# A hybrid attention and S5 block on one core: parameter scratch beside the query tiles, eigenvalue powers in the S5 stage, modulation weights two loads ahead

## The chip, the cores and the metric

The kernel runs on one core of one Trainium2 chip. The metric is the device time of one execution in microseconds (us). The core has a matrix engine (TensorE, PE in the profile), a vector engine (VectorE, DVE), a scalar engine (ScalarE, ACT), a general engine (GpSimd, POOL), a sync engine (SyncE, SP) that here only issues transfers, and 16 DMA engines that all queues share.

## The reference, cut to what matters

Two layers work on 512 latent and 256 context tokens of width 1024. Layer one is a latent attention with 16 heads, a SiLU gate and a residual norm. Layer two is a bidirectional S5 state-space layer with a gated linear unit. Each layer is modulated by a condition vector: shift, scale and gate come from a product of the silu of the condition with `w_mod`.

```python
sh, sc, gt = jnp.split(cond @ w_mod[i] + b_mod[i], 3, axis=-1)
h_lat = x * (1.0 + sc[:, None]) + sh[:, None]
# layer 1 (S5), for each direction, 128 groups, 64 states
lam_dt = lam * dt[:, None]
lam_bar = jnp.exp(lam_dt)
b_bar = ((lam_bar - 1.0) / lam)[..., None] * bmat
# x[t] = lam_bar * x[t-1] + b_bar u[t];  y[t] = Re(C x[t])
```

The kernel takes eight tokens as one step of the S5 recurrence. It therefore needs the powers 0 to 8 of `lam_bar` for tables, and the powers 8, 16, 32, 64 and 128 for a tree over the context.

## The kernel before

All matrix products are three products of a high and a low part (`mm3`, L81 to L83). The stages in order of time are these.

**Front, 0 to about 62 us.** Four times (q = 0 to 3) `mod_part` (L576) multiplies six loads of layer one's modulation weights, and `h_make` (L597 to L602) then makes two of the eight input tiles (`hh`, `hl`). The list `wtile` names the buffer of each weight load: 16 loads go to buffers of `hh` and `hl`, seven to `M`, one to `pair`. Beside it `s5_params` runs on DVE and then on POOL. Its scratch (`arena`, `T1`, `keep`) lies in the tiles `Qh0`, `Qh1`, `Ql0`, `Ql1` and one tile `G`; its scratch `T2` lies in `ext`. On POOL it builds the powers 0 to 8 (`cmul`, six instructions of 128x128 at L237 to L242, sixteen times), and then the four higher powers by squaring (four more `cmul`), negated copies (L292) and five stores `lamd` (L293). After that the two `bk` tiles, which lie in `ext` as well, are cleared (L629).

**Gating, about 62 to 361 us.** The loop over m = 0 to 15 makes `gate(m)` (48 matmuls against `hh`, `hl`), and between gates it places other work. `tables(n)` builds n chunks of S5 tables, 20 of 32 (`S5IN`) in this stage. A chunk is ten POOL instructions: six on 128x512 that make `wo` (L356 to L361), two that make `b1`, `b2` (L366, L368) and two that write `bk` (L372). One chunk later come the chunk's lag products on PE (L325, L328, called the lag here), which read `wo` and `bk`; their result `ks` is stored in eight small transfers `kd` on SP's queue. The chunk's input `cb` is loaded on the same queue, one chunk ahead, into two buffers. `s5_coefs` (L301) turns the powers on PE at m = 1, and right behind it `queries()` makes `Qh`, `Ql` from `qd`. `mod_more`, called from m = 2 on, three times per m, loads the next 512 to 768 KB of modulation weights (`pair`, two buffers, on ACT's queue) and runs the step of the load before it (L103), 24 steps in all. `prep(0)` for the first head is placed at m = 11 to 15.

**Attention, about 361 to 800 us.** Sixteen heads of five units; the other 12 chunks are built in it, five per eight units, and then 32 input tables on POOL (L391 to L396).

**Output product, S5, GLU, final product, to 1746 us.** In S5 `lamt` is loaded from `lamd` and used by `tree` (L1197 to L1202) and `recur` (L1212). POOL has no work there.

The order on each engine is made ahead of time by a planner that runs the program against a cost model. In this trace the users of the PSUM tiles `mm` (gates, lags, turns) stand on PE in the order in which the program names them; the steps L103 write other PSUM tiles (`modps`) and stand ahead of where the program has them.

Of the kernel before, what the change touches and what calls it, by code (L numbers as in the profile page):

```python
# [9 lines left out]
F32 = mybir.dt.float32  # L10
F32R = mybir.dt.float32r
I32 = mybir.dt.int32
AF = mybir.ActivationFunctionType
ALU = mybir.AluOpType
# [4 lines left out]
P = 128  # L19
D = 1024  # L20
KC = D // P
TL, TC = 512, 256
T = TL + TC
# [8 lines left out]
def hybrid_mla_s5(ctx, tc, I, O):  # L32
# [7 lines left out]
    def f(ap):  # L40
        return ap.bitcast(F32)
# [104 lines left out]
    G, Gd = [], {}  # L146


    GR, NCH, S5IN, WO = 128, 32, 20, [3]
    lamd = dram.tile([P, 5, 3, GR], F32, name="lamd")  # L150
    pind = dram.tile([8, GR, 2, P], F32, name="pind")
# [3 lines left out]

    def s5_params(take, take2, T2, pw, cci):

        def slots(k, take=take):
            return take()[:, :k * GR].rearrange("p (s g) -> p s g", g=GR)

        arena = [slots(6) for _ in range(3)]
        n = [0]
# [23 lines left out]
        A, S, M = ALU.add, ALU.subtract, ALU.mult  # L186
        T1, keep = slots(6), slots(6)

# [46 lines left out]

        def cmul(dr, di, ar, ai, br, bi, t1, t2, eng=pool):
            eng.tensor_tensor(t1, ar, br, op=M)  # L237
            eng.tensor_tensor(t2, ai, bi, op=M)
            eng.tensor_tensor(dr, t1, t2, op=S)
            eng.tensor_tensor(t1, ar, bi, op=M)  # L240
            eng.tensor_tensor(t2, ai, br, op=M)
            eng.tensor_tensor(di, t1, t2, op=A)  # L242

        lre, lim, lbr, lbi, cr, ci = (keep[:, i, :] for i in range(6))
        dt, den = cr, T2[:, 4, :]
# [29 lines left out]
        cps = [cps[k // 3][:, 2 * (k % 3):2 * (k % 3) + 2, :] for k in range(8)]  # L275
        lt = [arena[l // 2][:, 3 * (l % 2):3 * (l % 2) + 3, :] for l in range(5)]
        pk = [T1[:, 1:3, :], T1[:, 3:5, :], T2[:, 3:5, :]]
        p = pk[0]
        pool.memset(p[:, 0, :], 1.0)
        pool.memset(p[:, 1, :], 0.0)  # L280
        for k in range(8):
            pool.tensor_copy(pw[0:64, :, k, :], p[0:64])
            pool.tensor_copy(pw[64:128, :, 7 - k, :], p[64:128])
            cmul(cps[k][:, 0, :], cps[k][:, 1, :], p[:, 0, :], p[:, 1, :], clr, cli, t1, t2)
            q = lt[0] if k == 7 else pk[(k + 1) % 3]
            cmul(q[:, 0, :], q[:, 1, :], p[:, 0, :], p[:, 1, :], lbr, lbi, t1, t2)
            p = q
        for l in range(1, 5):
            a = [lt[l - 1][:, 0, :], lt[l - 1][:, 1, :]]
            cmul(lt[l][:, 0, :], lt[l][:, 1, :], *a, *a, t1, t2)  # L290
        for l in range(5):
            pool.tensor_scalar_mul(lt[l][:, 2, :], lt[l][:, 1, :], -1.0)  # L292
            pool.dma_start(out=lamd[:, l], in_=lt[l])  # L293
        return cps
# [121 lines left out]
    with ExitStack() as ctx_:  # L416
# [119 lines left out]
        with mkpool(name="in_h", bufs=KC) as hp, mkpool(name="in_w", bufs=3) as wp, \  # L536
# [17 lines left out]

            wtile = iter(["hh", "hl"] * KC + ["M"] * 7 + ["pair"])
            gmes = ExitStack()
# [63 lines left out]

            names = iter(("Qh0", "Qh1", "Ql0", "Ql1", "G"))

            def place():
                n = next(names)
                return (gv if n == "G" else qkv).tile([P, T], F32, name=n)
            cps = s5_params(place, lambda: gv.tile([P, T], F32, name="G"),
                            ext[:, 3 * GR:].rearrange("p (s g) -> p s g", g=GR), pw, cci)
# [109 lines left out]
            dve.tensor_sub(Cl, ckv, f(Ch))  # L737

            Qh, Ql = [], []

            def queries():
                for i in range(2):
                    Qh.append(qkv.tile([P, T], F32R, name=f"Qh{i}"))
                    Ql.append(qkv.tile([P, T], F32R, name=f"Ql{i}"))
                    dve.tensor_copy(Qh[i], qd[i])
                    dve.tensor_sub(Ql[i], qd[i], f(Qh[i]))
            rows1, steps1 = mod_steps(1, 0, 384, pair, ps, work, 0)
# [11 lines left out]
            def mod_more():  # L759

                n = next(done)
                ends.get(n - 2, lambda: None)()
                if ready:
                    ready.pop()()
                for load, step in itertools.islice(steps, 1):
                    load()
                    ready.append(step)
            todo = iter(range(S5IN))

            def tables(n):  # L770
                for c in itertools.islice(todo, n):
                    chunk(s5in, mm, c, S5IN - 1)
            prep0 = dict(zip(range(11, HEADS), prep(0)))
            for m in range(HEADS):
                for _ in gate0 if m == 0 else gate(m):
                    if m >= 2:
                        mod_more()
                if m >= 2:
                    mod_more()
                if m == 1:  # L780
                    s5_coefs(cps, mm, t512)
                    queries()
                for fn in prep0.pop(m, ()):
                    fn()
                tables(2 if m == 0 else 1 + (m % 4 == 2))
            spill()
# [350 lines left out]
    lamt = stp.tile([P, 5, 3, GR], F32, name="lamt", bufs=1)  # L1137
    sp.dma_start(out=lamt, in_=lamd)

    ues, (up,) = pools(dict(name="u_s", bufs=2))  # L1140
    us, scs = {}, {}

    def u_tile(m):
# [396 lines left out]
```

## Time and profile before

| what | us |
|---|---|
| three timed runs | 1749.81, 1754.17, 1759.38 |
| median | 1754.17 |
| profiled execution, its own time | 1748.03 |
| its span, first to last instruction | 1746.0 |
| PE busy in it | 1560.3 (89%) |
| POOL busy in it | 650.2 (37%) |

The span is cut in 40 slices of 43.65 us in the page's second part, with the busy share of each engine in tenths. A wait is put down to what released it. Spans of POOL are rough, and ends of matmuls are modelled.

### The profile page before, as it was taken

The numbers are of one execution on the slowest core, as the hardware profiler recorded it, in microseconds if no ns is written. First come the engines' busy times: TensorE is split into PE (matmuls) and PEld (weight loads), VectorE is DVE, ScalarE is ACT, GpSimd is POOL, SyncE is SP. The second block draws the span as 40 slices with busy tenths as digits, with TensorE's granted clock in tenths as the row PEclk, the third lists the DMA queues.
The fourth block names the chain that finished last, engine by engine and source line by source line (L and its number), as shares of the span: only waits on it lengthen the run. The fifth ranks groups of instructions, "written<-read, shape, count | busy, mean of one in ns | idle before, by whom it ended". The sixth has DMA issues, their size and how long they took to land.

```text
span 1746.0 us, 26883 instructions
## 1 busy us (share of the span) xinstructions
PE 1560.3 (89%) x9870; PEld 1305.9 (75%) x9870; DVE 962.8 (55%) x2502; ACT 729.9 (42%) x1253; POOL 650.2 (37%) x686
## 2 busy tenths in 40 slices
PE   6925978889889889999999999999779999999997
PEld 4713856678778778888888999888568888888876
DVE  7441322347758778785453488899853333333336
ACT  2411211246556556674224766766563222222220
POOL 3997777969948889970000000000000000000022
PEclk7966989999989999999999999999889999999999
DMA  9245676453356665654326767487452333333342
GB/s 326 79 139 185 209 230 201 137 194 120 115 159 196 203 193 195 200 181 158 115 69 196 240 221 233 141 333 282 155 212 89 119 108 108 109 108 109 135 155 73
DMA packets 156733, 293.60 MB, mean 168 GB/s; under 512 B 55069, under 2 KB 86217, under 8 KB 155577
## 3 DMA queue, kind: packets, MB, share of 16 engines
q1 hardware_dynamic: 104112, 235.84, 40.4%
q10 hardware_dynamic: 52104, 55.03, 10.4%
q8 instruction: 78, 1.28, 0.3%
q0 software_dynamic: 384, 1.01, 0.2%
q14 instruction: 55, 0.44, 0.1%
HBM read 230.39 MB, written 69.55 MB: 172 GB/s over the span
## 4 chain that ended last, share of the span: by engine, by line
PE 57%; DMA 14%; DVE 12%; POOL 6%; ACT 5%; issue 3%; SPq 2%; ACTq 0%; DVEq 0%; POOLq 0%
PE mm L81 16%; PE mm L83 16%; PE mm L82 16%; PE mm L1167 3%; DMA pair<-in_w_mod_dram 3%; DMA wraw<-in_wout_dram 2%; DMA cb<-in_CB_dram 1%; DMA toed<-kd 1%; DMA pw<-in_Bc_dram 1%; PE tr L858 1%; DMA ext<-pind 1%; DVE wlo L65 1%; DMA wraw<-in_win_dram 1%; PE modps L103 1%; POOL wo L359 1%
## 5 line engine op out<-in xcount | busy, mean ns | idle before, releaser
L65 DVE TENSOR_TENSOR wlo<-wraw,whi 128x1024 fp32r<-128x1024 f32 (+1 forms) x155 | 178.5, 1153 | 338.4 <-ACT whi L65 336.7
L1404 POOL TENSOR_TENSOR x<-x,row_g 128x1024 f32<-128x1024 f32 x4 | 11.3, 2829 | 926.0 <-DMA x<-x1d 926.0
L65 ACT CAST whi<-wraw 128x1024 fp32r<-128x1024 f32 (+1 forms) x155 | 149.2, 964 | 397.2 <-PE mm L82 262.9
L81 PE MATMUL mm<-st,whi 128*128 128x512 f32 x512 | 204.5, 399 | 5.4 <-ACT st L76 5.2
L83 PE MATMUL mm<-st,wlo 128*128 128x512 f32 x512 | 202.4, 395 | 0.0
L82 PE MATMUL mm<-st,whi 128*128 128x512 f32 x512 | 201.0, 393 | 0.5 <-DVE st L77 0.5
L81 PE MATMUL mm<-h,whi 128*128 128x512 f32 (+1 forms) x384 | 138.6, 362 | 0.2 <-DVE bnmv L950 0.2
L82 PE MATMUL mm<-h,whi 128*128 128x512 f32 (+1 forms) x384 | 137.1, 358 | 0.8 <-DVE h L1110 0.8
L83 PE MATMUL mm<-h,wlo 128*128 128x512 f32 (+1 forms) x384 | 136.6, 356 | 0.0
L81 PE MATMUL mm<-hh,whi 128*128 128x512 f32 (+1 forms) x320 | 113.4, 366 | 8.1 <-ACT whi L65 4.6
L81 PEld LDWEIGHTS mm<-st,whi 128*128 128x128 f32 x512 | 97.4, 190 | 26.8 <-ACT st L76 6.4
L82 PEld LDWEIGHTS mm<-st,whi 128*128 128x128 f32 x512 | 97.3, 190 | 23.2 <-DVE st L77 1.5
L83 PEld LDWEIGHTS mm<-st,wlo 128*128 128x128 f32 x512 | 97.2, 190 | 22.7
L82 PE MATMUL mm<-hl,whi 128*128 128x512 f32 (+1 forms) x320 | 113.0, 355 | 0.0
L83 PE MATMUL mm<-hh,wlo 128*128 128x512 f32 (+1 forms) x320 | 111.4, 352 | 0.0
L834 ACT ACTIVATE p<-sc,mx 128x768 f32<-128x768 f32 (+1 forms) x96 | 73.5, 766 | 37.7 <-DVE mx L833 35.3
L65 DVE TENSOR_TENSOR ptl<-tr,pth 128x384 fp32r<-128x384 f32 (+1 forms) x160 | 79.1, 524 | 15.4 <-ACT pth L65 14.5
L65 ACT CAST pth<-tr 128x384 fp32r<-128x384 f32 (+1 forms) x160 | 68.9, 462 | 40.9 <-PE tr L858 34.2
L833 DVE TENSOR_REDUCE mx<-sc 128x1 f32<-128x768 f32 (+1 forms) x96 | 73.8, 771 | 15.6 <-PE sc L823 14.4
L81 PEld LDWEIGHTS mm<-h,whi 128*128 128x128 f32 x384 | 72.9, 190 | 11.9 <-issue 0.7
L82 PEld LDWEIGHTS mm<-h,whi 128*128 128x128 f32 x384 | 73.1, 190 | 10.9 <-DVE h L1110 1.1
L83 PEld LDWEIGHTS mm<-h,wlo 128*128 128x128 f32 x384 | 72.9, 190 | 10.4
(377 smaller groups left out, 4188.0 us busy)
## 6 DMA issues: line engine op xcount, KB each, us to landing
wraw<-in_wglu_dram SPq DMA_DIRECT2D x64, 512.0 KB
wraw<-in_win_dram SPq DMA_DIRECT2D x36, 512.0 KB
wod<-wo SPq DMA_DIRECT2D x32, 512.0 KB
pw<-in_Bc_dram SPq DMA_DIRECT2D x32, 512.0 KB
pt<-wid SPq DMA_DIRECT2D x32, 512.0 KB
wo<-wod SPq DMA_DIRECT2D x32, 512.0 KB
pair<-in_w_mod_dram ACTq DMA_DIRECT2D x16, 768.0 KB
wo<-pind SPq DMA_DIRECT2D x21, 512.0 KB
```

Source lines behind the costliest of these rows:

```text
L65: return act.copy(hi, src).ins, (eng or dve).tensor_tensor(lo, src, f(hi), op=ALU.subtract).ins
L81: pe.matmul(ps, lh, rh, start=first, stop=False)
L82: pe.matmul(ps, lh, rl, start=False, stop=False)
L83: pe.matmul(ps, ll, rh, start=False, stop=last)
L103: pe.matmul(mps[32 * j:32 * j + 2, :n], sT[:, kc, :], w[:, n * j:n * j + n], start=(kc == 0), stop=(kc == KC - 1))
L359: pool.tensor_tensor(wi, cr, pi, op=ALU.mult)
L833: dve.reduce_max(mx[:, 1:2], s, axis=AX.X, negate=True)
L834: act.activation(p[:, a:b], s, AF.Exp, bias=mx[:, 1:2], scale=1.0, accum_out=mx[:, 2:3])
L858: pe.transpose(tp[:, n, :], p[:, j * P:(j + 1) * P], ident)
L1167: pe.matmul(o[:, r, 96 * q:96 * (q + 1)], wi[:, q, r, :], us[m][:, 4 * (c % 2) + q, :], start=True, stop=True)
L1404: pool.tensor_tensor(x, x, rows["g0"], op=ALU.mult)
```

## The change

- `s5_params` gets another place for its scratch: `T1` and the kept values lie in three tiles of `ls` (`xp0`, `xp1`, `xp0`), the arena in `Qh0`, `Qh1`, `Ql0`. One tile `G` less is taken.
- On POOL only the power 8 is stored, by one transfer. The powers 16 to 128 and the negated copies are made in the S5 stage, on POOL, from the loaded power 8, with a new scratch tile `lsc`.
- `Qh`, `Ql` are made in line, ahead of the loop over m.
- `wtile` names four loads for `hh`, `hl` and then a cycle of seven `M` and two `pair`, so that buffers of `M` and `pair` are used again within the front.
- `mod_more` is called from m = 0 on, and a step runs two loads after its own.
- `S5IN` is 19; `tables` builds none at m = 0, then one per m and one more at m = 3, 7, 11, 15. `s5_coefs` moves to m = 4.

```diff
-    GR, NCH, S5IN, WO = 128, 32, 20, [3]
-    lamd = dram.tile([P, 5, 3, GR], F32, name="lamd")
+    GR, NCH, S5IN, WO = 128, 32, 19, [3]
+    lamd = dram.tile([P, 2, GR], F32, name="lamd")
...
-        T1, keep = slots(6), slots(6)
+        X = [slots(4, take4) for _ in range(3)]
+        T1 = X[0]
...
-        lre, lim, lbr, lbi, cr, ci = (keep[:, i, :] for i in range(6))
+        lre, lim, cr, ci, lbr, lbi = (X[1 + i // 4][:, i % 4, :] for i in range(6))
...
-        lt = [arena[l // 2][:, 3 * (l % 2):3 * (l % 2) + 3, :] for l in range(5)]
-        pk = [T1[:, 1:3, :], T1[:, 3:5, :], T2[:, 3:5, :]]
+        pk = [T1[:, 1:3, :], X[2][:, 2:4, :], T2[:, 3:5, :]]
...
-            q = lt[0] if k == 7 else pk[(k + 1) % 3]
+            q = pk[(k + 1) % 3]
...
-        for l in range(1, 5):
-            a = [lt[l - 1][:, 0, :], lt[l - 1][:, 1, :]]
-            cmul(lt[l][:, 0, :], lt[l][:, 1, :], *a, *a, t1, t2)
-        for l in range(5):
-            pool.tensor_scalar_mul(lt[l][:, 2, :], lt[l][:, 1, :], -1.0)
-            pool.dma_start(out=lamd[:, l], in_=lt[l])
+        pool.dma_start(out=lamd, in_=p)
...
-            wtile = iter(["hh", "hl"] * KC + ["M"] * 7 + ["pair"])
+            wtile = itertools.chain(["hh", "hl"] * 2, itertools.cycle(["M"] * 7 + ["pair"] * 2))
...
-            def queries():
-                for i in range(2):
-                    Qh.append(qkv.tile([P, T], F32R, name=f"Qh{i}"))
...
+            for i in range(2):
+                dve.tensor_copy(Qh[i], qd[i])
+                dve.tensor_sub(Ql[i], qd[i], f(Qh[i]))
...
-                ends.get(n - 2, lambda: None)()
-                if ready:
-                    ready.pop()()
+                ends.get(n - 3, lambda: None)()
+                if len(ready) == 2 or n > 24 and ready:
+                    ready.pop(0)()
...
                 for _ in gate0 if m == 0 else gate(m):
-                    if m >= 2:
-                        mod_more()
-                if m >= 2:
                     mod_more()
-                if m == 1:
+                    mod_more()
+                if m == 4:
                     s5_coefs(cps, mm, t512)
-                    queries()
...
-                tables(2 if m == 0 else 1 + (m % 4 == 2))
+                tables((m > 0) + (m % 4 == 3))
...
-    sp.dma_start(out=lamt, in_=lamd)
+    sp.dma_start(out=lamt[:, 0, 0:2], in_=lamd)
...
+    lsc = up.tile([P, 2, GR], F32, name="lsc", bufs=1)
+    for l in range(5):
+        if l:
+            a = [lamt[:, l - 1, r] for r in range(2)]
+            cmul(lamt[:, l, 0], lamt[:, l, 1], *a, *a, lsc[:, 0], lsc[:, 1])
+        pool.tensor_scalar_mul(lamt[:, l, 2], lamt[:, l, 1], -1.0)
```

## Rows read from the trace of the kernel before

**Rows 1.** The page, part 2: busy tenths in 40 slices of the span.
```profile
PE   6925978889889889999999999999779999999997
POOL 3997777969948889970000000000000000000022
```
**Rows 2.** Busy time by stretch: PE, PEld, DVE, ACT, POOL (instructions), clock, DMA share, GB/s.
```profile
107.00:149.00 42.00, 10.22 (x56) 0.77 (x56) 2.21 (x3) 0.00 (x0) 41.33 (x65) 0.50 0.56 176
153.00:354.00 201.00, 167.24 (x1486) 133.30 (x1479) 53.04 (x101) 42.24 (x98) 153.83 (x172) 0.91 0.61 192
...
361.00:481.00 120.00, 105.24 (x1001) 92.55 (x1000) 83.05 (x172) 67.78 (x163) 106.65 (x122) 0.99 0.45 147
...
915.00:970.00 55.00, 51.95 (x310) 45.69 (x310) 17.02 (x29) 27.54 (x53) 0.00 (x0) 0.97 0.65 204
```
**Rows 3.** Waits of PE, 95 to 153 us, then two of 160 to 430 us.
```profile
PE modps L103 <- DMA pair<-in_w_mod_dram: 46.5, 8, 12.1
...
PE mm L325 <- POOL wo L358: 12.3, 4, 5.0
PE mm L325 <- POOL wo L361: 11.6, 4, 5.1
```
**Rows 4.** PE in order of time: start, duration, line, names, idle before and releaser.
```profile
95.02 0.28 PE L83 MATMUL mm<-hh,wlo 128*128 128x256 f32 x1
...
152.01 1.46 PE L103 MATMUL modps<-pair,sT 128*2 128x384 f32 x8 [5.23 <-DMA pair<-in_w_mod_dram]
153.24 1.08 PE L325 MATMUL mm<-wo,ext 128*32 128x128 f32 x16
...
182.60 0.50 PE L81 MATMUL mm<-hh,whi 128*128 128x512 f32 x1 [1.06 <-DVE Gs L712]
...
190.97 0.28 PE L83 MATMUL mm<-hh,wlo 128*128 128x256 f32 x1
```
**Rows 5.** POOL in order of time, with the same columns.
```profile
124.50 0.45 POOL L242 TENSOR_TENSOR Qh<-Ql,ext 128x128 f32<-128x128 f32 x1
...
126.13 0.40 POOL L237 TENSOR_TENSOR Ql<-Qh 128x128 f32<-128x128 f32 x1
...
146.36 0.41 POOL L629 MEMSET ext<- 128x384 f32 x1
146.72 0.61 POOL L293 DMA_DIRECT2D lamd<-Ql  x1
147.35 1.76 POOL L372 TENSOR_TENSOR ext<-b,b 64x128 f32<-64x128 f32 x2
...
361.33 1.52 POOL L882 MEMSET kz<- 64x768 f32 x2 [6.95 <-issue]
```
**Rows 6.** Groups of POOL instructions, 107 to 147 us: busy, mean ns, idle before.
```profile
L358 POOL TENSOR_TENSOR wo<-wo,wt 128x512 f32<-128x512 f32 x3 | 3.8, 1265 | 0.0
...
L357 POOL TENSOR_TENSOR wt<-cb,pw 128x512 f32<-128x512 f32 x3 | 3.3, 1093 | 0.0
```
**Rows 7.** The same view, 147 to 360 us, with the releasers of idle time.
```profile
L372 POOL TENSOR_TENSOR ext<-b,b 64x128 f32<-64x128 f32 x40 | 21.0, 525 | 11.8 <-PE mm L325 10.2
...
L356 POOL TENSOR_TENSOR wo<-cb,pw 128x512 f32<-128x512 f32 x17 | 19.0, 1116 | 33.3 <-DMA cb<-in_CB_dram 28.4 <-PE modps L103 4.6
```
**Rows 8.** The chain that ended last, two loads of chunk input: start, duration.
```profile
222.30 6.18 DMA cb<-in_CB_dram
...
341.91 2.26 DMA cb<-in_CB_dram
```
**Rows 9.** Instructions on the tile lamt: duration min/median/max, first and last start.
```profile
L1197 DVE TENSOR_TENSOR tr<-sc,lamt x8: 692/692/694, 970.3 to 1129.1; 128x512 f32<-128x512 f32 x8
...
L1138 SPq DMA_DIRECT2D lamt<-lamd x1: 327/327/327, 915.0 to 915.0; - x1
```
**Rows 10.** Transfers issued on SP's queue in the front: start, time of all.
```profile
10.35 7.04 SPq L571 DMA_DIRECT2D M<-in_w_mod_dram  x7
...
19.73 2.63 SPq L571 DMA_DIRECT2D hh<-in_w_mod_dram  x3
```

More of the change, by code (lines that the diff above doesn't have):

```diff
@@ L154, in hybrid_mla_s5, with cmul, s5_params @@
     toed = [dram.tile([P, 16, P], F32, name=f"toed{i}") for i in range(8)]
-    def s5_params(take, take2, T2, pw, cci):
+    def cmul(dr, di, ar, ai, br, bi, t1, t2):
+        pool.tensor_tensor(t1, ar, br, op=ALU.mult)
+        pool.tensor_tensor(t2, ai, bi, op=ALU.mult)
+        pool.tensor_tensor(dr, t1, t2, op=ALU.subtract)
+        pool.tensor_tensor(t1, ar, bi, op=ALU.mult)
+        pool.tensor_tensor(t2, ai, br, op=ALU.mult)
+        pool.tensor_tensor(di, t1, t2, op=ALU.add)
+    def s5_params(take, take2, take4, T2, pw, cci):
         def slots(k, take=take):
@@ L234, in cossin @@
             return co, so
[L236 to L242, printed above, removed]
-        lre, lim, lbr, lbi, cr, ci = (keep[:, i, :] for i in range(6))
+        lre, lim, cr, ci, lbr, lbi = (X[1 + i // 4][:, i % 4, :] for i in range(6))
         dt, den = cr, T2[:, 4, :]
@@ L619, in proj @@
                 return out
[L621 to L626, printed above, removed]
+            names, places = iter(("Qh0", "Qh1", "Ql0")), iter((0, 1, 0))
+            cps = s5_params(lambda: qkv.tile([P, T], F32, name=next(names)), lambda: gv.tile([P, T], F32, name="G"),
+                            lambda: ls.tile([P, TL], F32, name=f"xp{next(places)}", bufs=2),
                             ext[:, 3 * GR:].rearrange("p (s g) -> p s g", g=GR), pw, cci)
@@ L737, in hybrid_mla_s5 @@
             dve.tensor_sub(Cl, ckv, f(Ch))
-            Qh, Ql = [], []
-            def queries():
-                for i in range(2):
-                    Qh.append(qkv.tile([P, T], F32R, name=f"Qh{i}"))
-                    Ql.append(qkv.tile([P, T], F32R, name=f"Ql{i}"))
-                    dve.tensor_copy(Qh[i], qd[i])
-                    dve.tensor_sub(Ql[i], qd[i], f(Qh[i]))
+            Qh = [qkv.tile([P, T], F32R, name=f"Qh{i}") for i in range(2)]
+            Ql = [qkv.tile([P, T], F32R, name=f"Ql{i}") for i in range(2)]
+            for i in range(2):
+                dve.tensor_copy(Qh[i], qd[i])
+                dve.tensor_sub(Ql[i], qd[i], f(Qh[i]))
             rows1, steps1 = mod_steps(1, 0, 384, pair, ps, work, 0)
```

## The prediction

> **What bounds the kernel now.** I read the slices first. PE is at eight tenths or more nearly everywhere after slice 8, but its third slice (87 to 131 us) stands at 2 tenths, the fourth at 5, and POOL is at 9 and 7 there [rows 1]. That hole is the largest single loss of the trace, so I read the stages by stretch, then the waits of PE, then PE and POOL in order of time.
>
> The hole runs from the last matmul of gate 0 at 95.3 to the first lag at 153.2, which is 58 us [rows 4]. In 107 to 149 us PE is busy 10.2 of 42 us at a granted clock of 0.50 while POOL is busy 41.3 [rows 2]. The waits name eight loads of modulation weights, 46.5 us in all [rows 3]; but these are steps that stand in the hole because PE had nothing else. What the program has next on PE is the lag of chunk 0, and every later gate stands behind it. That lag reads `bk`, whose first write on POOL is at 147.35 and takes 1.76 to 149.1 [rows 5]. `bk` lies on the scratch of the power calculation, so it is cleared (146.36) only when the last power is done. So POOL sets the end of the hole, and the last step, at 152.01, adds 4 us.
>
> After the hole, in 153 to 354 us, PE is busy 167 of 201 us and POOL 154 [rows 2]. Neither is full. PE waits 23.9 us for POOL's `wo` in eight waits [rows 3], and POOL waits 28.4 us for loads of `cb`, 10.2 us for lags to free `bk` and 4.6 us behind a step [rows 7]. The two engines run a loop through SP's queue: lag, stores `kd`, load `cb`, `wo`, lag. Attention begins at about 361, where its first POOL instruction stands [rows 5].
>
> **The change part by part.**
>
> *Powers.* Between 126.13 and 147.35 POOL spends 21.2 us [rows 5]. In it lie four `wo` instructions of chunk 2, 2 x 1.27 and 2 x 1.09 = 4.7 us [rows 6], one clear of 0.41 and one of the five stores at 0.63 (start of the store to start of the next instruction), which stay [rows 5]. Removed: 21.2 - 4.7 - 0.4 - 0.6 = 15.5 us. The first `bk` is then ready at 149.1 - 15.5 = 133.6, or at 128.9 if the four `wo` instructions come after it. I take 131. The single store now reads a place that the second clear overwrites, so that clear waits for a landing; chunk work stands beside it, and without that cover I bound it by 6.2, the longer landing in [rows 8].
>
> *Order of gates and lags.* With no tables at m = 0, gates 1 and 2 stand ahead of lag 0. A gate takes 182.60 to 191.25 = 8.65 us [rows 4], so 17.3 us of gates move into the hole, from 95.3 to about 113. The remaining 18 us take about four steps at 1.46 us, the half-clock price of [rows 4]. The queries no longer wait for the stores of powers (their tiles are not used for them), so both `pair` buffers are free from then on. This matters only through the steps.
>
> *What is left from 131 us on, POOL.* A chunk is ten instructions; 153.8 us for 172 of them is 8.94 us per chunk [rows 2]. Of 19 chunks 2.5 are done by 131, so 16.5 x 8.94 = 147.5 us. POOL's idle time in 153 to 354 is 201 - 153.8 = 47 us. All of it kept gives 131 + 147.5 + 47 = 326; none gives 279. I keep the waits for `cb` (28.4 us, the loop through SP is as long as before) and the small rest (47 - 28.4 - 10.2 - 4.6 = 4 us), and drop the two waits for PE, which is now ahead. That gives 131 + 147.5 + 32 = 311.
>
> *What is left, PE.* From 153.2 to 361 are 208 us. Taken away are two gates (17.3) and one lag (1 us); added are about four steps, since eight of the 24 stood in the hole and four do now, 4 x 0.73 = 3 us (half of 1.46, for the full clock). So 193 us with PE's idle time as it is (201 - 167 = 34), and 159 without it: 324 or 290. POOL's 311 lies between, and the last lags now stand behind gate 15, so nothing but the last lag follows POOL: attention begins at about 312 instead of 361. That is 49 us earlier; bounds 290 and 327, or 71 and 34 us.
>
> *The thirteenth chunk in attention.* POOL is busy 106.7 of 120 us in 361 to 481 [rows 2], so another 8.94 us has little room there. It lies at the end of the chunks, and the input tables start one unit later with it. Nothing is the lower bound, 9 us the upper; I take 4.
>
> *Powers in the S5 stage.* `lamt` is loaded at 915.0 and first read by the tree at 970.3 [rows 9]. POOL does nothing in between, DVE is busy 17 of 55 us [rows 2]. The same instructions took 15.5 us; twice that is still under 53 us after a landing of 2.3 [rows 8]. Cost 0. If the cover were gone, the tree would be late by the excess, and the recurrences behind it.
>
> *Front.* Today seven loads of `M`, which are needed last, are issued at 10.35, and the second group's `hh` loads only at 19.73 [rows 10]. The new list loads in the order of use, so the input tiles come earlier. Against it, DVE makes tiles 2 and 3 before the parameters are done, not after. PE's gain here falls into the hole, since POOL's chain sets lag 0; a slip of POOL's chain counts in full. I take 0, between -4 and +4, the length of those four DVE instructions, put at about 1 us each as an estimate: a DVE product over 512 columns takes 0.69 us [rows 9], and these have 768.
>
> *Sum.* 49 - 4 = 45 us. The profiled execution's own time is 1748.0 (span 1746.0 and 2.0 around it), which gives 1703. The median of the runs, 1754.2, lies 6.1 above that execution; I carry half of it and forecast 1706.
>
> **The rivals.**
>
> *The `cb` loads get slower (A).* With two weight loads in flight at all times, small loads land late: `cb` took 6.18 us at 222 us, with steps running, and 2.26 us at 342, after the last [rows 8]. If each of eight chunks loses 3.9 us, 31 us go, and with the thirteenth chunk at 9 the gain is 49 - 31 - 9 = 9; with half of it 24. Time 1727 to 1742. For it: `cb` already is POOL's largest wait. Against it: the 24 loads are the same, only spread further.
> The Trainium skill says the same of all queues (Trainium Kernel Development and Optimization, section Key Constraints): transfers from SP, ACT and POOL run on the same 16 DMA engines and interleave. By that rule alone the deeper prefetch only moves bytes ahead of `cb`, and the sum would be A's; the two landings above agree with it, but the number of late ones is open.
>
> *The loop goes without waits (B).* Attention begins at 290, PE's bound: 71 - 4 = 67 us, 1684, down to 1675. For it: PE comes to each lag later than POOL. Against it: gates 8 to 15 have no steps left beside them, so POOL at 1.25 chunks per gate (11.2 us) is slower than PE (8.65) there.
>
> *Only the gates move (C).* The planner fills POOL's freed time with later chunks' `wo`, lag 0 stays near 149, and the chunks end as now: 17 us from the gates, less 9 for the thirteenth chunk, 8 us or 1743, and 1754 if the loop loses as much again. It would not do what it says.
>
> *Slower (D).* The steps are called from m = 0 on and stand out of program order, each with a wait of about 4.9 us for its load as in the hole (46.5 less the first, by seven) [rows 3]. There the wait cost nothing, as POOL was late. If the planner puts them in a row ahead of the gates, PE stands still while the gates could run. Sixteen steps beyond the hole cost 78 us and the kernel takes 1784; it decides from the tenth such wait on (45 / 4.9). Against it: both buffers are free, and a load issued two calls ahead has one gate half more to land in.
>
> **How the numbers follow.** Forecast (1688 to 1726) 0.55, A 0.17, B 0.11, C 0.08, D 0.09. The range 1682 to 1745 takes in the forecast, A, a part of B and C, together 0.8. About 0.5% (9 us) is what a measurement of this kernel can tell from no change. Faster by more than that: forecast, A and B, 0.83; same: C, 0.08; slower: D, 0.09.
>
> **What would show it.** Right: no PE hole longer than some 20 us between 95 and 135, the first L325 near 131, the first attention instruction near 312, POOL waits on `cb` near 28 us, the powers on POOL done well ahead of the first tree. Wrong: a first lag after 140 (C), L103 waits on `pair` of more than 20 us outside the hole (D), `cb` landing near 6 us on each chunk (A), or an attention stage longer than the present 439 us (361 to about 800), which would give the gain back.

## The result, and the profile after

The changed kernel takes 1719.69 us (median of four runs, 1717.50 to 1721.97) against 1751.99 for the kernel before, run beside it (four runs, 1746.29 to 1759.38). The ratio is 0.9834, with a 95% interval of 0.9801 to 0.9868. The profiled execution takes 1721.6 us with a span of 1719.5, where before had 1748.0 and 1746.0: 26.4 us less by the one profiled execution of each, 32.3 by the medians.

The slices of the page, PE and POOL, answer to [rows 1]:
```profile
PE   7867979499889999799999999999679999999997
POOL 2999958859679989940021000000000000000022
```
The hole in PE's third slice is gone (2 tenths before, 6 now). There is a new one: PE's eighth slice, which begins at 301 us, stands at 4 where POOL stands at 8. The windows show both, with the columns of [rows 2]:
```profile
107.00:149.00 42.00, 24.34 (x212) 11.92 (x213) 4.16 (x5) 5.26 (x12) 40.41 (x58) 0.67 0.76 259
153.00:354.00 201.00, 155.95 (x1357) 126.29 (x1356) 58.20 (x114) 47.63 (x112) 157.15 (x177) 0.88 0.63 199
...
300.00:331.00 31.00, 8.52 (x131) 6.99 (x129) 2.38 (x6) 3.80 (x8) 30.21 (x36) 0.65 0.39 120
885.00:940.00 55.00, 51.84 (x304) 45.24 (x303) 20.17 (x37) 25.53 (x52) 16.29 (x29) 0.94 0.54 170
```
From 300 to 331 us PE is busy 8.5 of 31 us and POOL 30.2. No gate is left, and what PE waits for is `wo`. In order of time on PE, first the lag of chunk 0, then the last three lags of this stage and the first score of attention:
```profile
134.58 1.46 PE L103 MATMUL modps<-pair,sT 128*2 128x384 f32 x8 [1.17 <-DMA pair<-in_w_mod_dram]
136.15 1.08 PE L320 MATMUL mm<-wo,ext 128*32 128x128 f32 x16
...
313.95 0.65 PE L320 MATMUL mm<-wo,ext 128*32 128x128 f32 x8 [7.76 <-POOL wo L356]
...
324.50 0.66 PE L320 MATMUL mm<-wo,ext 128*32 128x128 f32 x8 [9.71 <-POOL wo L353]
...
329.78 0.65 PE L320 MATMUL mm<-wo,ext 128*32 128x128 f32 x8 [4.62 <-POOL wo L356]
331.26 0.80 PE L803 MATMUL sc<-Ch,pair 128*128 128x512 f32 x1 [0.64 <-DVE ks L327]
```
Lag 0 comes at 136.15 (153.24 before, [rows 4]), and the first score at 331.3, where the same matmul (L819) of before comes at 362.9. That is 31.6 us earlier. The same stretch on POOL:
```profile
39.20 0.52 POOL L157 TENSOR_TENSOR xp<-xp,xp 128x128 f32<-128x128 f32 x1 [1.19 <-issue]
...
135.11 0.98 POOL L367 TENSOR_TENSOR ext<-b,b 64x128 f32<-64x128 f32 x2
...
310.11 1.50 POOL L866 MEMSET kz<- 64x768 f32 x2
...
360.04 0.45 POOL L367 TENSOR_TENSOR ext<-b,b 64x128 f32<-64x128 f32 x1 [22.75 <-PE mm L320]
```
The first `bk` is written at 135.11, not 147.35 as in [rows 5]. The clear of `kz`, which marked the start of attention in [rows 5], now lies at 310.1, 21 us ahead of the first score: POOL works ahead into attention while PE waits for it, and then stands 22.75 us itself until PE has reached a lag of attention.

Attention takes about as long as before. The output projection's first matmul comes at 756.8 against 784.6, `lamt`'s load at 887.2 against 915.0, the first tree at 943.4 against 970.3 [rows 9], and the span ends 26.5 us earlier. Nothing that was won at 331 is lost behind it but 3.8 us in attention and 1.3 in the last stages.

### The profile page after: what moved, and what is told of

It reads as the page before. It is cut to its first block, busy times and chain, and to the rows that moved or that the text cites. A ratio compares the mean times of both kernels' runs of the same rounds, so it can differ in the third digit from the quotient of the medians.

```text
span 1719.5 us, 26866 instructions
## 1 busy us (share of the span) xinstructions
PE 1558.3 (91%) x9870; PEld 1301.2 (76%) x9870; DVE 966.9 (56%) x2502; ACT 728.7 (42%) x1253; POOL 652.0 (38%) x682
## 3 DMA queue, kind: packets, MB, share of 16 engines
q10 hardware_dynamic: 52104, 55.03, 10.7%
## 4 chain that ended last, share of the span: by engine, by line
PE 59%; POOL 12%; DMA 10%; DVE 9%; ACT 4%; issue 3%; SPq 1%; ACTq 0%; POOLq 0%; DVEq 0%
PE mm L81 16%; PE mm L83 16%; PE mm L82 16%; PE mm L1157 3%; PE tr L842 2%; DMA wraw<-in_wout_dram 2%; DMA ext<-pind 2%; PE mm L1291 1%; DMA cb<-in_CB_dram 1%; POOL wo L356 1%; DMA toed<-kd 1%; POOL wo L354 1%; POOL wo L353 1%; POOL wt L355 1%; POOL wt L352 1%
## 5 line engine op out<-in xcount | busy, mean ns | idle before, releaser
L65 DVE TENSOR_TENSOR wlo<-wraw,whi 128x1024 fp32r<-128x1024 f32 (+1 forms) x155 | 179.1, 1157 | 327.7 <-ACT whi L65 324.4
L81 PE MATMUL mm<-hh,whi 128*128 128x512 f32 (+1 forms) x320 | 109.6, 355 | 7.3 <-ACT wmod L299 5.4
L82 PE MATMUL mm<-hl,whi 128*128 128x512 f32 (+1 forms) x320 | 109.4, 344 | 0.0
L65 DVE TENSOR_TENSOR ptl<-tr,pth 128x384 fp32r<-128x384 f32 (+1 forms) x160 | 78.7, 522 | 17.9 <-ACT pth L65 17.2
L65 ACT CAST pth<-tr 128x384 fp32r<-128x384 f32 (+1 forms) x160 | 68.1, 462 | 37.9 <-PE tr L842 31.6
L817 DVE TENSOR_REDUCE mx<-sc 128x1 f32<-128x768 f32 (+1 forms) x96 | 73.6, 770 | 18.4 <-PE sc L807 17.3
```

The costliest lines, as they stand in the source:

```text
L65: return act.copy(hi, src).ins, (eng or dve).tensor_tensor(lo, src, f(hi), op=ALU.subtract).ins
L81: pe.matmul(ps, lh, rh, start=first, stop=False)
L82: pe.matmul(ps, lh, rl, start=False, stop=False)
L817: dve.reduce_max(mx[:, 1:2], s, axis=AX.X, negate=True)
```

## The experiments

All have been run against the kernel before, on one chip for each group of runs. The table is read from their traces. *PE busy* is its busy time in 0 to 150 us, *PE idle* its idle time from 150 us to the first score, both from the windows; *out* is the first matmul of the output projection, and the ratio has its interval in brackets.

| kernel | first bk | PE busy | PE idle | first score | out | ratio to before |
|---|---|---|---|---|---|---|
| before | 147.4 | 81.4 | 35.8 | 362.9 | 784.6 | 1 |
| after | 135.1 | 114.0 | 42.6 | 331.3 | 756.8 | 0.9834 [0.9801, 0.9868] |
| after, powers back on POOL | 150.1 | 107.1 | 37.8 | 337.1 | 763.7 | 0.9885 [0.9857, 0.9913] |
| after, old front | 132.5 | 104.7 | 42.2 | 339.4 | 766.1 | 0.9875 [0.9856, 0.9893] |
| after, old order of chunks | 133.8 | 96.7 | 32.9 | 349.2 | 773.4 | 0.9891 [0.9830, 0.9952] |
| after, loads one ahead | 135.2 | 114.7 | 30.2 | 320.6 | 747.1 | 0.9800 [0.9770, 0.9830] |
| before, powers moved | 128.5 | 92.8 | 33.6 | 352.7 | 772.5 | 0.9937 [0.9915, 0.9960] |
| before, powers moved, cb on POOL | 130.0 | 95.8 | 26.8 | 339.5 | 760.8 | 0.9856 [0.9808, 0.9904] |
| after, cb on POOL | 137.8 | 113.6 | 37.8 | 331.9 | 769.8 | 0.9901 [0.9869, 0.9934] |
| after, two wo | 132.3 | 114.7 | 35.0 | 325.2 | 751.6 | 0.9838 [0.9786, 0.9890] |
| after, two wo, one ahead | 133.3 | 113.7 | 33.8 | 327.6 | 756.1 | 0.9807 [0.9763, 0.9852] |
| after, two wo, cb two ahead | 132.1 | 113.6 | 34.0 | 330.6 | 753.9 | 0.9842 [0.9812, 0.9872] |
| after, 17 chunks in gating | 135.6 | 113.0 | 18.0 | 308.0 | 756.2 | 0.9802 [0.9762, 0.9842] |
| after, 17 chunks, tables on DVE | 134.6 | 113.2 | 21.2 | 309.0 | 786.2 | 0.9983 [0.9959, 1.0008] |

**The parts of the change, undone one at a time.** The first puts the work of the powers back on POOL ahead of the chunks; its results are unused, and the S5 stage still makes its own.
```diff
         pool.dma_start(out=lamd, in_=p)
+        for l in range(4):
+            q = pk[(l + 1) % 3]
+            cmul(q[:, 0, :], q[:, 1, :], p[:, 0, :], p[:, 1, :], p[:, 0, :], p[:, 1, :], t1, t2)
+            p = q
+        for l in range(5):
+            pool.tensor_scalar_mul(t1, p[:, 1, :], -1.0)
```


> The kernel after, with the 24 products and 5 scalings of the higher powers done a second time on POOL where they stood before (their results unused; the S5 stage keeps its own). Theory (the gain is POOL's freed 15.5 us, because POOL's chunks set the end of the gating stage): the first bk goes from 135 to about 150, gates 1 and 2 still run before lag 0, and attention's first score goes from 331 to 343-347; time 1732-1736, ratio to the kernel before about 0.990. Rival (the gain comes from the order of loads in the front, the deeper prefetch or the chunk less): no change, 1718-1722, ratio 0.982.

It takes 1730.03 us, ratio 0.9885. The first `bk` moves by 15.0 us to 150.1, as it should, but the first score only by 5.8:
```profile
L373 POOL TENSOR_TENSOR ext<-b,b x64: 443/455/1436, 150.1 to 458.8; 64x128 f32<-64x128 f32 x64
```
The point estimates differ by 0.0051, some 9 us, and the two intervals overlap by a little (0.9857 to 0.9868). So the freed time is worth something, against the rival, but less than half of it reaches attention, against my number. In the kernel with the powers back PE stands idle less later on: 37.8 us from 150 us to the first score, where after has 42.6.

The second run gives the front's loads the tiles they had before.
```diff
-            wtile = itertools.chain(["hh", "hl"] * 2, itertools.cycle(["M"] * 7 + ["pair"] * 2))
+            wtile = iter(["hh", "hl"] * KC + ["M"] * 7 + ["pair"])
```


> The kernel after with the front's weight loads in the tiles of before (16 in query-tile buffers, then M, then pair). Theory (the new order of loads makes query tiles 2 and 3 early, which puts their DVE work and a DVE wait of 2.4 us for the first modulation part ahead of the parameter chain): POOL's first product goes from 39.2 back to about 33.5, the first bk from 135 to about 129, attention's first score from 331 to 325-331; time 1713-1720. Rival (the new order itself gives a part of the gain, as the front ends earlier): 1722 or more.

It takes 1729.73 us: the rival's number, and my theory of this part falls. POOL's chain does start earlier (first `bk` 132.5), yet the first score comes 8.1 us later. The reason stands in the first 150 us, of this kernel and then of after:
```profile
0.00:150.00 150.00, 104.72 (x691) 78.80 (x692) 81.62 (x180) 42.45 (x61) 114.68 (x170) 0.87 0.56 186
```
```profile
0.00:150.00 150.00, 113.95 (x722) 75.86 (x723) 79.44 (x178) 43.99 (x65) 110.01 (x166) 0.89 0.62 209
```
PE's busy time (the first figure in front of a bracket) is 9.2 us less by 150 us. A late start of PE was not absorbed by the hole.

The third lays the chunks as before; that puts lag 0 back ahead of gates 1 and 2, and the 20th chunk back into gating.
```diff
-    GR, NCH, S5IN, WO = 128, 32, 19, [3]
+    GR, NCH, S5IN, WO = 128, 32, 20, [3]
...
-                if m == 4:
+                if m == 1:
...
-                tables((m > 0) + (m % 4 == 3))
+                tables(2 if m == 0 else 1 + (m % 4 == 2))
```


> The kernel after with the chunks where they were laid before (two after gate 0, then one a gate and one more after gates 2, 6, 10, 14, 20 in all, coefficients after gate 1). Theory (lag 0 then stands ahead of gates 1 and 2 on TensorE and leaves the hole up to 136 empty, and the 20th chunk is one more ahead of attention): TensorE's hole before lag 0 is back, first score 331 goes to 340-350, time 1728-1738. Rival (POOL sets the end whatever TensorE does before 136): first score 331-335, time 1718-1722.

It takes 1731.86 us, and the first score comes at 349.2, 17.9 us later: as the theory expected, and the rival falls. PE has done 17.3 us less by 150 us, the length of the two gates that I counted. The run moves the gates and the 20th chunk together, so the 17.9 us at the first score are not shown to be the gates' alone. The ratios differ by 0.0057, about 10 us, and the interval of this run is wide.

The fourth takes the extra distance from the modulation loads.
```diff
-                ends.get(n - 3, lambda: None)()
-                if len(ready) == 2 or n > 24 and ready:
-                    ready.pop(0)()
+                ends.get(n - 2, lambda: None)()
+                if ready:
+                    ready.pop()()
```


> The kernel after with layer two's modulation loads one step ahead instead of two. Theory (the steps now stand in the hole before lag 0 or beside POOL's chunks, where TensorE has time): waits of the steps rise from 17.8 us to 25-45 us, the hole takes most, time 1718-1724. Rival (the deeper prefetch is what gives the gain): waits of 35 us or more of which most reach the end, 1738-1750.

It takes 1718.10 us, not to be told from after. PE's waits for `pair` in 95 to 340 us are 23.5 us, with 23.2 in after. The deeper prefetch brings nothing here. In the trace the first score is even 10.7 us earlier, and POOL's order of work shows why. Up to the last lag POOL has begun 191 instructions of chunks in this kernel and 205 in after, where 19 chunks are 190. So in after 15 instructions of attention's own chunks stand ahead of the last lag, here one. The stretch from 135 us to the last lag, of after and then of this kernel (POOL is the fifth engine):
```profile
135.00:329.80 194.80, 152.49 (x1401) 122.26 (x1394) 50.55 (x96) 39.88 (x93) 166.81 (x192) 0.89 0.61 190
```
```profile
135.00:319.80 184.80, 153.52 (x1394) 123.58 (x1390) 51.13 (x96) 40.16 (x93) 156.72 (x178) 0.91 0.63 198
```
POOL is busy 10.1 us less, and the stretch is 10.0 us shorter.

**One part alone.** The kernel before with nothing but the powers moved to the S5 stage:
```diff
-        for l in range(1, 5):
-            a = [lt[l - 1][:, 0, :], lt[l - 1][:, 1, :]]
-            cmul(lt[l][:, 0, :], lt[l][:, 1, :], *a, *a, t1, t2)
...
-            pool.dma_start(out=lamd[:, l], in_=lt[l])
+        pool.dma_start(out=lamd, in_=lt[0][:, 0:2])
```


> The kernel before with one part of the change alone: the higher powers moved to the S5 stage (front, order of chunks and prefetch as before). Theory (POOL's freed time is worth what putting it back cost, and the order of gates and chunks is a gain by itself): first bk goes from 147 to 132, lag 0 from 153 to 138, first score from 363 to 352-357; time 1740-1747. Rival (every us of POOL's earlier start arrives, as in the forecast's sum): 1733-1737. Rival that the powers cost the S5 stage something: 1750 or more.

It takes 1740.22 us, ratio 0.9937, and the first score moves by 10.2 us to 352.7: the first theory, not the sum of the forecast, by which the whole 18.9 us of POOL's earlier start should have come through. The trace shows where they went. POOL waits 33.7 us for `cb` up to 331 us; the longest of these waits, on POOL and then on SP's queue:
```profile
184.92 1.28 POOL L356 TENSOR_TENSOR wo<-wo,wt 128x512 f32<-128x512 f32 x1
199.42 1.95 POOL L351 TENSOR_TENSOR wo<-cb,pw 128x512 f32<-128x512 f32 x1 [13.22 <-DMA cb<-in_CB_dram]
```
```profile
182.93 4.44 SPq L311 DMA_DIRECT2D toed<-kd  x7
187.41 1.15 SPq L330 DMA_DIRECT2D kd<-ks  x1
188.60 0.48 SPq L331 DMA_DIRECT2D kd<-ks  x1
195.05 0.30 SPq L330 DMA_DIRECT2D kd<-ks  x1
195.40 0.42 SPq L331 DMA_DIRECT2D kd<-ks  x1
196.27 0.30 SPq L330 DMA_DIRECT2D kd<-ks  x1
196.62 0.42 SPq L331 DMA_DIRECT2D kd<-ks  x1
197.13 0.37 SPq L339 DMA_DIRECT2D cb<-in_CB_dram  x1
```
POOL is free at 186.2. The load that it needs is issued at 197.13 and there 2.3 us later. Ahead of it on the queue stand eight copies `toed` and the stores of a lag, and SP itself stands from 189.1 to 195.05; by the waits that is for the copies to land (6.0 us). In 110 to 350 us SP stands 29.0 us in seven waits for `ks`, the result of a lag on PE, and 14.2 us in seven for `toed`. This load is not slow; it is issued late. SP also stands 51.2 us in six waits until POOL frees a buffer for the next `cb`, and the stores behind such a load stand with it. To test the late issue, one line of this kernel was changed:
```diff
-            sp.dma_start(out=cbs[c], in_=I["CB"][:, 4 * c:4 * c + 4])
+            pool.dma_start(out=cbs[c], in_=I["CB"][:, 4 * c:4 * c + 4])
```


> The kernel before with the higher powers moved, as in the run of that part alone, and the loads of cb issued from POOL's queue instead of SP's. Theory (with the powers gone POOL starts 18.9 us earlier, but its next cb stands in SP's queue behind the stores of the last lag, which wait for TensorE: 33.7 us of cb waits up to 331 take most of it back): cb waits fall below 5 us, for 17 issues of 0.6 us, first score from 352.7 to 330-342, time 1722-1733. Rival (POOL then waits for TensorE itself, for a free bk, or TensorE's own work sets attention's start): POOL's waits for the lags grow from 10.6 to 25 us or more, first score 346 or later, time 1735-1744.

It takes 1723.67 us, ratio 0.9856, with the first score at 339.5: both inside what the theory expected. POOL's waits in 131 to 331 us, largest first:
```profile
POOL wo L351 <- DMA wod<-wo: 8.0, 2, 6.1
POOL ext L367 <- PE mm L320: 6.8, 4, 3.5
POOL ext L367 <- DMA pair<-in_w_mod_dram: 2.3, 1, 2.3
```
No `cb` wait is left among them, and the waits for lags do not take their place, as the rival had it (10.6 in the run without this edit, 6.8 in this). These two edits alone come within 4 us of the whole change. The edit also takes the wait for a free `cb` buffer out of SP's queue, so that the stores behind it can go earlier; no run separates the two effects.

The Trainium skill (Trainium Kernel Development and Optimization, section Key Constraints) has it that to issue from several engines only saves the issue time of the sequencer, since all transfers run on the same 16 DMA engines. Here the measurement says more: the 13.2 us at the first score are a matter of place in the order, not of issue time, since an issue took 0.36 us on SP and the load no longer shares a queue with stores that wait for a lag or a copy.

**Attempts to take the loop's idle time out of the kernel after.** The same edit there:

> The kernel after with the loads of cb issued from POOL's queue instead of SP's. Theory (15.0 us of POOL's waits in gating are cb loads behind other issues of SP): the waits fall below 4 us, 19 issues of 0.6 us cost 11 of it, first score 331 goes to 322-330, time 1712-1720. Rival (the waits move to the lags, or the mixing of the next chunk into the last two keeps the tail): first score 330-336, time 1718-1726.

It takes 1731.63 us, worse than either expectation. Waits for `cb` are 7.9 us instead of 15.0, the first score is where it was (331.9), and attention becomes 12.4 us longer. Each issue takes POOL's own time, 0.58 us in the median of 32, and POOL's last table of attention ends at 764.7 instead of 749.8. Ten issues lie in attention and take 5.8 of these 14.9 us; what makes the rest is not shown. PE then waits for values of the output stage, and the chain that ended last leads from POOL's last product over its store on SP's queue to the load of output weights behind that store:
```profile
763.45 1.23 POOL wo L391
...
764.70 0.32 SPq L400
...
765.07 3.33 DMA wraw<-in_wout_dram
...
768.42 0.62 ACT whi L65
```
```profile
769.84 2.50 PE L81 MATMUL mm<-whi,vh 128*128 128x512 f32 x5 [10.33 <-ACT vh L76]
```
Two `wo` buffers in gating, so that POOL can't mix the next chunk's products into the last ones:
```diff
-    GR, NCH, S5IN, WO = 128, 32, 19, [3]
+    GR, NCH, S5IN, WO = 128, 32, 19, [2]
```


> The kernel after with two wo buffers instead of three in the gating stage. Theory (POOL runs ahead into the first chunk of attention and mixes its products with those of the last two chunks of gating, so that the last lag waits 9.7 and 4.6 us for wo): the last lag comes at 318-322 instead of 329.8, time 1708-1714. Rival (the third buffer is what keeps POOL busy over the waits for cb, and the tail is POOL's sum of work whatever its order): last lag at 330 or later, time 1718-1730.

With 1722.35 us it can't be told from after. The last lag comes at 324.4, between the two expectations, the first score at 325.2. The edit did not do what it was made for: up to the last lag POOL has begun 204 instructions of chunks, where after has 205. In the profiled execution the span is 1713.6, but the timed runs don't bear that out: inconclusive. With the loads one step ahead as well:

> The kernel after with both: two wo buffers in gating and the modulation loads one step ahead. Theory (one ahead left the last lag at 319.8 because its order mixed less of the next chunk into the last two, so the two edits remove the same wait): no more than the better of the two alone, last lag at 315-320, time 1706-1713. Rival (one ahead gains by something of its own, such as earlier cb loads): 1700 or less.

1718.27 us: no better than one ahead alone, as expected, though above the time that I gave. The last lag, at 326.2, is later than with one ahead alone (319.8). POOL has begun 191 instructions of chunks up to it, as with one ahead alone, but has been idle 35.0 us since 135 us where that kernel has 28.1. So running ahead is one thing that moves the tail, and POOL's waits are another; what made them longer here is not shown. And with two `wo` buffers and `cb` loaded two chunks ahead:
```diff
-            cbs[c] = work.tile([P, 4, 2, 32], F32, name="cb", bufs=2)
+            cbs[c] = work.tile([P, 4, 2, 32], F32, name="cb", bufs=3)
...
-        if c not in cbs:
-            load(c)
-        if c < end:
-            load(c + 1)
+        for n in range(c, min(c + 2, end) + 1):
+            if n not in cbs:
+                load(n)
```


> The kernel after with two wo buffers in gating and three cb buffers, loaded two chunks ahead from SP's queue. Theory (12 us of cb waits are left with two wo buffers; a load two chunks ahead passes the stores that held it up, and costs POOL no issue): cb waits below 4 us, first score from 325.2 (two wo buffers alone) to 314-321, time 1706-1714. Rival (what follows a free POOL is a wait for bk or wo, that is for TensorE's lags): first score 323-328, time 1714-1724.

1720.54 us, first score 330.6: a miss. POOL still waits 10.0 us for `cb`, where two `wo` buffers alone left 12.0, and besides for lags and stores. Neither edit frees POOL of `cb` in this kernel (7.9 and 10.0 us are left), so whether that would gain anything here stays untested.

**Fewer chunks ahead of attention.** `S5IN` is 17 instead of 19:
```diff
-    GR, NCH, S5IN, WO = 128, 32, 19, [3]
+    GR, NCH, S5IN, WO = 128, 32, 17, [3]
```


> The kernel after with 17 chunks instead of 19 in the gating stage, the other two in attention. Theory (POOL's chunks set the end of gating: TensorE waits 22 us for wo between 306 and 331 with no gate left to do, and attention hides a chunk): with two chunks of 9.3 us less, attention's first score comes at 312-318 and attention takes the two at no cost; time 1700-1708, ratio about 0.972. Rival (a chunk in attention costs 4 us or more, or attention's start is bound by something else): 1715-1728.

The first half of the theory holds: the first score comes at 308.0, 23.3 us earlier, and PE's idle time ahead of it falls from 42.6 to 18.0 us. The second half falls: 1718.49 us, no gain that can be told, because attention gives all of it back at its end.
```profile
731.64 0.38 PE L81 MATMUL mm<-oh,uh 128*128 128x256 f32 x1 [0.23 <-DVE ol L65]
756.23 0.80 PE L81 MATMUL mm<-whi,vh 128*128 128x512 f32 x1 [21.24 <-ACT vh L76]
```
POOL's last table ends at 747.8 and the values `vh` that PE waits for are begun at 748.2, which looked to me like a wait for the tables. The chain that ended last says otherwise. On ACT `vh` stands behind five casts of output weights, and these wait for their loads, which go through two buffers one after the other:
```profile
729.50 9.37 DMA wraw<-in_wout_dram
...
740.46 2.62 DMA wraw<-in_wout_dram
...
745.02 2.65 DMA wraw<-in_wout_dram
...
748.31 5.88 ACT vh L76 x8
```
So a second chain ends where attention ends, and here it is the loads of output weights. In after the first of these loads is issued at 750.26, right behind the store of the last table (749.82), and the output projection starts at 756.8; an attention that ended earlier would meet them there, though no run shows it. On my reading of that time, that POOL's tables were the chain, every fourth table of the kernel with 17 chunks was given to DVE, with scratch of its own:
```diff
+                    dv = len(early) % 4 == 3
-                    win_early(tabs, lambda: [work.tile([P, 4, P], F32, name=f"wt{k}", bufs=1) for k in (1, 2)],
-                              [pool], i < len(units) - 7)
+                    win_early(tabs, lambda: [work.tile([P, 4, P], F32, name=f"wt{k + 2 * dv}", bufs=1) for k in (1, 2)],
+                              [dve if dv else pool], i < len(units) - 7)
```


> The kernel after with 17 chunks in gating, as in the run of that alone, and with every fourth of the 32 window tables of attention made by DVE with scratch of its own instead of by POOL. Theory (attention ends with the later of two chains: TensorE's, some 410 us behind the first score, and POOL's last table; with 17 chunks TensorE waited 21 us for values that stood behind POOL's tables): POOL's last table comes 40 us or more earlier, the wait of 21.2 us is gone, the 23 us by which attention starts earlier reach the S5 stage, lamt's load comes at 862-872 instead of 888, time 1692-1704. Rival (those 21 us are of attention itself, or DVE's 8 tables, some 25 to 35 us of its time, hold up the softmax as much): lamt's load at 878 or later, time 1708-1722.

It takes 1749.42 us: this costs all that the change had won, and both expectations missed it. The wait of PE for `vh` is gone, but attention is longer. The waits of POOL and of DVE in 300 to 800 us, and the two largest of PE in attention, say why:
```profile
POOL wt L386 <- DMA pw<-in_Bc_dram: 101.6, 15, 20.6
```
```profile
DVE wt L386 <- DMA pw<-in_Bc_dram: 30.6, 5, 12.2
```
```profile
PE tr L842 <- DVE ptl L65: 28.9, 12, 11.2
PE mm L81 <- DVE G L860: 21.1, 12, 7.9
```
A table waits for its input on the engine that makes it. On DVE the work of attention stands behind it: PE's two waits above are 3.0 and 7.3 us with 17 chunks and all tables on POOL. POOL then waits too, 101.6 us for `pw` where that kernel has 23.6; that this is because the tables go through few buffers in turn is how I read it, and no run tests it. So the link from POOL's last table to the end of attention is shown where `cb` is on POOL. With 17 chunks the 21 us belong to the loads of output weights, and no run takes these away by themselves.

## Why the prediction was right, and where its steps were not

The forecast was 1706 in a range of 1682 to 1745, and faster at 0.83. The time, 1719.7, lies in it and in the forecast's own range, though the gain, 32.3 us by the medians, is two thirds of the 48 between before's median and the forecast. None of the rivals came about as a whole. Lag 0 is not late (C). PE's waits for `pair` behind the hole are 5.4 us in all, 1.8 at most (D). The loop kept most of its idle time: POOL is idle 28.0 us from the first `bk` to the last lag (B). `cb` waits shrank to 15.0 us instead of growing (A). A's mechanism does show in one place of after: of the longest of these waits, 9.4 us, 4.5 are late issue (POOL is free at 237.6, the load is issued at 242.08) and 4.9 are landing, and the next load takes 8.0 us to land:
```profile
247.01 1.11 POOL L351 TENSOR_TENSOR wo<-cb,pw 128x512 f32<-128x512 f32 x1 [9.38 <-DMA cb<-in_CB_dram]
```
```profile
242.08 0.38 SPq L339 DMA_DIRECT2D cb<-in_CB_dram  x1
```
```profile
243.02 7.96 DMA cb<-in_CB_dram
```

- *Powers, 15.5 us of POOL.* Right: put back, they move the first `bk` by 15.0.
- *Powers in the S5 stage at nothing.* Right: POOL does them from 889.9 to 907.5, the first tree comes at 943.4, and from `lamt`'s load to the end of the span it takes 832.3 us where before took 831.0.
- *Gates 1 and 2 into the hole, 17.3 us.* Right: with the old order PE has done 17.3 us less by 150. The first score comes 17.9 later, with the 20th chunk back as well.
- *The thirteenth chunk, 4 us.* Right: from the first score to the output projection the four kernels with 12 chunks take 421.8 us on average (419.8 to 424.2), the seven with 13 and no wait for `vh` 426.2 (423.3 to 428.5).
- *Front, 0, between -4 and +4.* Wrong, and in its reasoning, which put a term at nothing that was worth something. POOL's chain slipped by 5.9 us (its first product 33.31 before, 39.20 now, above): besides the four instructions for tiles 2 and 3, the parameters now stand behind a copy on DVE that waits for the first part of the modulation. The first product of before, and then this copy:
```profile
33.31 0.51 POOL L237 TENSOR_TENSOR Ql<-G 128x128 f32<-128x128 f32 x1 [1.89 <-issue]
```
```profile
23.60 0.42 DVE L573 COPY modrow<-modps 128x256 f32<-128x256 f32 x1 [2.37 <-PE modps L571]
```
  But I said that PE's gain in the front falls into the hole. It doesn't: gates and steps fill the hole, so what PE does early stays won. Undone, the front costs 8.1 us at the first score in spite of the earlier `bk`, and by the ratios 0.0041, some 7 us. That the forecast came as near as it did is in part luck: this gain, which it did not have, makes up for a part of what the next step missed.
- *Attention begins at 312, bounds 290 and 327.* This is the step that failed; it came at 331.3, and only `kz`, the mark I had named, came at 310.1. The sum was 131 + 147.5 + 32. Measured up to the last lag, by the window shown above for after: POOL starts `bk` at 135.1, is then busy 166.7 us and idle 28.0, to 329.8. The start is 4 late; the front explains 2.6 of it (132.5 with the old front). The idle time is 4 less than I kept, though less of it is `cb` and more has no releaser in the profile:
```profile
L351 POOL TENSOR_TENSOR wo<-cb,pw 128x512 f32<-128x512 f32 x18 | 19.9, 1106 | 23.2 <-DMA cb<-in_CB_dram 15.0 <-issue 7.9
```
  The term that failed is the work, 19 us more than 147.5. A product is not slower: 1106 ns here, 1116 for the same one (L356) in [rows 7]. There are more instructions: from 135.1 on POOL begins 188 of chunks, where 16.5 chunks are 165. Fifteen are attention's own, nine products and six small ones, made ahead and mixed into the last chunks of gating. Eight are small ones (`b1`, `b2`, `bk`) of the 2.5 chunks that I had taken as done by 131; of those only the products and one pair of `b1`, `b2` were. The two clears, `kz` and `bk`, add 1.9 us. The kernel with the loads one ahead, where POOL does not run ahead, has its last lag 10.0 us earlier. I had counted the work that the stage needs, not what POOL would be given to do before its end.

The sum of 45 us was thus 31.6 - 3.8 - 1.3 = 26.5 in the span. By the table the 31.6 come apart in another way: PE does 32.6 us more up to 150 us, has 38.5 us less to do after it up to the first score (138.7 against 177.1), and is idle 6.9 us more there. The other kernels read the same way: in eight of the twelve with 19 or 20 chunks in gating, the first score and PE's busy time up to 150 us add up to 444.1 to 445.9 us, and in the other four to 435.3 to 441.3. The loop of lag, store, load and `wo` behind the hole did not become shorter when POOL got ahead; what counted was how much PE had done when it began. POOL's 15.5 us count for what they let PE do in the hole, 6 to 10 us, and the order of the chunks and the front give the rest. Undone one at a time, the powers, the front and the order cost 5.8, 8.1 and 17.9 us at the first score, 31.8 together, and the whole is 31.6. That the parts are independent does not follow: the powers alone brought 10.2, and the fourth part, undone, moved the first score 10.7 the other way.

No run is better than the change by more than the measurement can tell. One ahead, 17 chunks, and two `wo` buffers with one ahead stand at 0.980 to 0.981, with intervals that overlap that of after.

## What to carry to other kernels

Time freed on an engine in a loop is worth what its partners can do with it: ask first which queue ties them, and whether the load that the freed engine needs next stands on that queue behind stores that wait for others. Before you count a stage by the work it needs, look at what the engine can run ahead into: the next stage's work can be mixed into the last items on which everybody waits. And an earlier start of a stage is a gain only if the chain that ends last there starts earlier too.

## What the runs showed that I had not expected

- A 128 KB load of `cb` issued from POOL takes 0.58 us of POOL's stream (median of 32), and 0.36 of SP's. In the kernel after, the 19 issues between 131 and 331 us take 10.9 us, more than the 7.1 by which the waits for `cb` fell.
- The products of a window table take about 1.3 us each on POOL and 0.69 on DVE, same shape and type. Yet the eight tables cost DVE more in waits (47.4 us, of which 30.6 are for `pw`) than in work (34.4).
- The granted clock went with the hole: it rose from 0.50 to 0.67 in 107 to 149 us, where PE now works, and stands at 0.65 in 300 to 331, where it now waits; before, 300 to 330 us had 1.00 (1 is 2.4 GHz, 0.5 is 1.2).
